# A two-layer decoder trunk on one core: GpSimd applies the gate operands' norm where they are stored, norm factors come two blocks at a time, and layer B's first weights are loaded and split another way

## The chip, the cores and the metric

The kernel runs on one core of one Trainium2 chip. Its engines are PE (TensorE matmul), PEld (its weight load), DVE (VectorE), ACT (ScalarE), POOL (GpSimd) and SP (SyncE, which here issues the DMAs). The metric is the device time of one execution in microseconds (us); the kernel before took 2546.34 us, the median of 3 runs.

## What is computed

2048 tokens of width 1024 go through two layers. Cut to what matters here:

```python
u = rmsnorm(x, norm_a_g)                       # layer A
q, k, v, f, gate = split(u @ w_in_a)           # widths 1024, 1024, 1024, 16, 1024
q, k = rmsnorm per head of 64 (q), (k)
o = fox_attention(q, k, v, log_sigmoid(f + b_forget))      # 16 heads, causal
h = x + (o * silu(gate)) @ w_out_a
k_s, v_s = split(rmsnorm(h, kv_norm_g) @ w_kv)             # 4 heads, shared keys and values
q, gate = split(rmsnorm(h, norm_b_g) @ w_in_b)             # layer B
o = swa_sink_attention(rope(rmsnorm(q)), rope(rmsnorm(k_s)), v_s, sinks)   # window 128
out = h + (o * silu(gate)) @ w_out_b
```

## The kernel before

Every matrix product is made in three matmuls: each operand is split into a high part of type fp32r and a low part with the rest, and high x high, high x low and low x high are added up in one PSUM bank. The norm of x has two factors. The gain of a column is multiplied into the weights when these are split (L396 on ACT makes `wh`, L397 on DVE makes `wl` from the raw weights in a slot of `wr`). The factor of a row, one over the root of the mean square, is not multiplied into x: it is kept in `factors` and applied to each product after the matmul.

`normer` (L478) loads x in 16 blocks of 128 tokens (`load_block`, slots of `st` and `wr` in turn), splits them into `uh` and `ul` (tiles of `big`) and works out the factor of each block: squares, a sum, and in `rstd` (L295) the steps L301 to L307, one set for each block.

`projections` makes layer A's products in seven groups of 6 or 8 heads (4 in the sixth): in each, all weights of the group are loaded and split, and a loop over the 16 blocks runs 24 matmuls (L663) into one of three banks `b`, norms the heads (`qk_norm`: L409 on ACT, L411, L301 to L307, L413 and L415 on DVE; L415 reads the bank last), transposes them on PE (L291, one block later) and stores them. The first group holds half of the values, the second and third the keys, the fourth to sixth the queries (the fourth also the forget gate), the seventh the other half of the values.

Layer A's gate isn't among the groups. Its product is made later, as filler work inside attention, so the groups carry `jobs` for it: in the second and third group its 1024 columns of weights are split and stored (`split_w`, 8 jobs), and in the fourth to seventh `uh` and `ul` are stored to `ut` in DRAM (`spill_u`, 16 jobs of one DMA of 1 MB each). A group does four jobs, at the blocks of `JOBS_AT`.

`attention_a` goes through 16 heads and four chunks of 512 queries. `gate` is a generator that `feed` advances by some matmuls at each step: for each chunk and each of 8 tiles of 128 gate columns it runs 24 matmuls L960 into the bank `pb` (in the tail into `sc`), from `ut` (slots `wh`, `wl`) and the stored weights (`wr`). Then L967 on DVE multiplies the bank by the row factors (`rows`, loaded from `rr` in DRAM), L968 on ACT takes tanh, L969 on DVE makes (1 + tanh) x product, and L970 stores it to `gt`. As the factor is in the product only once this way, the other place of silu's argument is made good elsewhere: `recips`, which inverts the sums of the softmax, multiplies them by the same factors (L816). A flag, `rest`, keeps `feed` still for one step after each gate tile. Attention's own DVE work is the running sums (L914), row maxima (L851, L856) and sums (L801); POOL subtracts high parts from weights of the softmax (L903).

`out_a` makes layer A's output projection: four chunks of 512 tokens, in each two halves of columns and four tiles of 128 tokens, with 24 matmuls L1171 and an evacuation L1175 that adds the residual (a slot of `qn`), stored to `h1` by L1176. While a chunk runs, `gated` multiplies the next chunk's attention output, sums and gate (L1122 on POOL, L1123, L1124 and L1126 on DVE). In the last chunk `last()` loads and splits layer B's first weights (`w_kv`: four loads L379 into `wr`, eight splits L396 and L397), and `norm` begins with the blocks of `h1`: a block is loaded, squared and summed on ACT (L503), transposed on PE (L291, in a bank of `b`) and split (L327, L328).

The order of the instructions on each engine comes from a scheduler that goes by priority, the pools' free slots and its own estimates; some instructions are held in program order.

Of the kernel before, what the change touches and what calls it, by code (L numbers as in the profile page):

```python
# [22 lines left out]
P = 128  # L23
S = 2048
D = 1024
# [33 lines left out]
JOBS_AT = (0, 3, 6, 9)  # L59
# [17 lines left out]
SLOTS = dict(big=8, st=4, wr=2, wh=9, wl=9, sq=2, qn=2, rows=1, rot=1, ro1=1, ro2=2)  # L77
# [13 lines left out]
class Trunk:  # L91
# [56 lines left out]
    def constants(self):  # L148
# [66 lines left out]
        self.gk16 = row("gk16", a["knorm_b_g"].rearrange("(o d) -> o d", o=1)[:, :ROT], ROT)  # L215

        self.late = [self.loads.pop()]
# [120 lines left out]
    def block_sums(self, sums, tb):  # L338

        nc = self.nc  # L340
        ps = self.ps(("pa", "pb")[tb % 2], [P, 1])
        self.tc.keep_in_program_order(
            nc.tensor.matmul(ps, sums, self.ones[:, :1], start=True, stop=True)
        )
# [11 lines left out]
    def weights(  # L356
# [16 lines left out]
        for dt in dts:  # L373
# [20 lines left out]
            else:  # L394
                g = gain[:, dt : dt + 1]
                nc.scalar.activation(h, raw, AF.Copy, scale=g)  # L396
                nc.vector.scalar_tensor_tensor(lo, raw, g, f_(h), ALU.mult, ALU.subtract)  # L397
# [4 lines left out]
        return hs, ls  # L402

    def qk_norm(self, ps, nh, tb, rope, r0):
# [5 lines left out]
        sm = self.sb("sm", [P, 4, 8], bufs=3)  # L410
# [50 lines left out]
    def factor_rows(self, i, ch):  # L461

        rows = self.sb("rows", [P, CH])
# [16 lines left out]
    def normer(self, src):  # L480
# [3 lines left out]
        uh, ul, blocks = {}, {}, {}  # L484
# [10 lines left out]
        def rstd(tb, sm, ss=None):  # L495
            self.rstd(sm, 1, D, ss=ss, out=factors[:, tb : tb + 1])

        def load(tb):
            blocks[tb] = xt = self.load_block(src, tb)
            if not turned:  # L500
                _, junk = parts(tb)
                sm = self.sb("sm", [P, 4, 8], bufs=3)
                nc.scalar.activation(  # L503
                    junk, xt.rearrange("p (c t) -> p c t", t=P), AF.Square,
                    accum_out=sm[:, 0, :1],
                )
                rstd(tb, sm)
# [14 lines left out]
        def factor(tb, dt):  # L522
            if turned and dt == 0:
                blocks[tb] = self.block_squares(blocks[tb])
            if turned and dt == FACTOR_AT:
                sm = self.sb("sm", [P, 4, 8], bufs=3)
                rstd(tb, sm, self.block_sums(blocks.pop(tb), tb))
# [3 lines left out]
    def projections(self, normed, groups, row, later=None, pre=None, hook=None, first=None):  # L531
# [45 lines left out]
        if later is not None:  # L577
            wg, cg, gain, spill, wsplit = later

            def spill_u(ch, k, c0):  # L580
                t = (uh, ul)[k]
                c = slice(c0, c0 + NDT // 2)
                tc.keep_in_program_order(
                    nc.sync.dma_start(
                        out=spill[ch, k, c].rearrange("c p t -> p c t"), in_=f_(t[ch][:, c])
                    )
                )

            def split_w(dt):
# [13 lines left out]
                partial(spill_u, ch, k, c0)  # L603
                for ch in range(NCH) for k in range(2) for c0 in (0, NDT // 2)
# [148 lines left out]
    def attention_a(self, w_out, result):  # L753
# [16 lines left out]

        factors = self.sb("ro1", [NCH * NSB, 2, 32])
# [34 lines left out]
        def recips(h, c0=0, c1=NCH):  # L806
# [9 lines left out]
            nc.vector.tensor_tensor(rc, rc, factors[:nr, 1 if c0 else 0], ALU.mult)  # L816
# [125 lines left out]
        def gate():  # L942


            for ch in range(NCH):
                rows, us = self.factor_rows(0, ch), []
# [4 lines left out]
                for ft in range(NDT):  # L951
# [15 lines left out]
                    nc.vector.tensor_tensor(g, ps, rows, ALU.mult)  # L967
                    nc.scalar.activation(g, g, AF.Tanh, scale=0.5)  # L968
# [18 lines left out]
        for c in range(2):  # L987
            nc.sync.dma_start(
                out=factors[: (NCH - c) * NSB, c],
                in_=d["rr"][0, c * CH :].rearrange("(b i) -> b i", i=32),  # L990
            )
# [17 lines left out]
        gate_bank, weight_slots, rest = "pb", cycle(["wr"]), False  # L1009
# [21 lines left out]
        def feed(n, pause=False):  # L1031


            nonlocal fed, rest
            if pause and rest:
                rest = False
# [445 lines left out]
```

## Time and profile before

| | |
|---|---|
| time, median of 3 runs | 2546.34 us (2545.75 to 2551.03) |
| profiled execution, its own time | 2548.29 us |
| its span, first to last instruction | 2546.4 us |
| mean granted TensorE clock | 0.993 |
| POOL busy | 938.7 us, 611 instructions |
| DVE busy | 1788.7 us, 4353 instructions |

The views used below: the page gives the busy time of each engine over the span, and the span in 40 slices with the busy share of each in tenths. A table of windows gives for each stretch its length, then the busy us (and instructions) of PE, PEld, DVE, ACT and POOL, the granted clock, the share of DMA and GB/s. A row of the timeline holds start, duration (of all that are put together), engine, line, operation, output <- input by the program's names, shape, how often, and in brackets the idle time before with what ended it. A group's row holds how often, then the busy us and the mean ns of one, then the idle time before by what ended it. A row of waits holds the total in us, how often, and the longest.

### The profile page before, as it was taken

The page shows a single profiled execution, that of the slowest core. Times are in us where ns is not written, and L with a number is a line of the kernel's source. Part 1 is how long each engine was busy: PE and PEld are TensorE (multiplying, and loading weights), DVE is VectorE, ACT ScalarE, POOL GpSimd, SP SyncE. Part 2 cuts the span into 40 slices and gives each one's busy share as a digit, 9 for nine tenths or more (in the row PEclk, how much of TensorE's full clock was granted, in tenths as well). Part 3 has the DMA queues.
Part 4 walks back from the last instruction along what each step waited for, and adds up shares of the span by engine and source line. Part 5 has one row for each costly group of instructions (what it writes and reads, how often), then busy time and mean ns, then how long its engine had stood idle before and what let it go on. Part 6 is the DMA issues. An engine that isn't in the chain of part 4 may idle for free. (4 is left out here: it accounts for less than half of the span.)

```text
span 2546.4 us, 37588 instructions
## 1 busy us (share of the span) xinstructions
PE 2474.7 (97%) x12320; PEld 2058.7 (81%) x12320; DVE 1788.7 (70%) x4353; ACT 1350.7 (53%) x2598; POOL 938.7 (37%) x611
## 2 busy tenths in 40 slices
PE   8999999999999999999999899989999999899999
PEld 6788899988878778877887677778888888688887
DVE  7656666726888889888888864436766422788885
ACT  5433333415777778777877631135332213777774
POOL 0000000014877778777877732200011000355552
PEclk9999999999999999999999999999999999999999
DMA  6656655687454654655466478845443424655541
GB/s 190 185 160 187 176 149 147 203 262 226 125 165 118 195 170 137 183 159 159 124 178 182 144 231 262 269 146 151 131 114 94 145 95 139 192 156 163 169 143 65
DMA packets 357155, 419.33 MB, mean 165 GB/s; under 512 B 65440, under 2 KB 248768, under 8 KB 350784
## 3 DMA queue, kind: packets, MB, share of 16 engines
q1 hardware_dynamic: 356960, 416.93, 56.0%
q8 instruction: 98, 1.61, 0.3%
q14 instruction: 97, 0.79, 0.1%
HBM read 265.29 MB, written 151.40 MB: 164 GB/s over the span
## 5 line engine op out<-in xcount | busy, mean ns | idle before, releaser
L663 PE MATMUL b<-wh,big 128*128 128x512 f32 (+3 forms) x2560 | 774.3, 376 | 13.2 <-ACT wh L396 12.8
L903 POOL TENSOR_TENSOR big<-st,big 128x1024 fp32r<-128x1024 f32 (+1 forms) x320 | 678.2, 2132 | 254.3 <-ACT big L902 164.6
L663 PEld LDWEIGHTS b<-wh,big 128*128 128x128 f32 x2560 | 473.9, 189 | 84.2 <-ACT wh L396 14.2
L663 PE MATMUL b<-wl,big 128*128 128x512 f32 (+3 forms) x1280 | 475.7, 372 | 1.1 <-DVE wl L397 0.9
L914 DVE TENSOR_TENSOR ac<-ac,st 128x512 f32<-128x512 f32 (+3 forms) x576 | 355.0, 616 | 48.4 <-ACT ac L906 23.9
L897 ACT ACTIVATE st<-sc 128x512 f32<-128x512 f32 (+1 forms) x512 | 277.4, 586 | 120.0 <-PE sc L889 71.2
L929 PE MATMUL pa<-big 128*128 128x512 f32 (+2 forms) x1280 | 333.0, 373 | 4.3 <-ACT sq L937 3.9
L902 ACT CAST big<-st 128x1024 fp32r<-128x1024 f32 (+1 forms) x320 | 302.5, 946 | 7.7
L663 PEld LDWEIGHTS b<-wl,big 128*128 128x128 f32 x1280 | 242.6, 190 | 37.4 <-DVE wl L397 4.9
L929 PEld LDWEIGHTS pa<-big 128*128 128x128 f32 x1280 | 225.0, 190 | 43.5 <-ACT sq L937 10.2
L888 PE MATMUL sc<-big 128*128 128x512 f32 (+2 forms) x640 | 246.1, 385 | 3.2 <-ACT st L897 1.9
L409 ACT ACTIVATE sq<-b,r 128x512 f32<-128x512 f32 (+2 forms) x128 | 77.8, 608 | 314.5 <-PE b L663 314.4
L889 PE MATMUL sc<-big 67*128 67x512 f32 (+2 forms) x640 | 236.3, 369 | 0.0
L851 DVE CUSTOM_DVE_ANT_0 mx<-mx,rot 128x128 f32<-128x128 f32 (+3 forms) x240 | 210.8, 878 | 34.9 <-PE mx L840 30.3
L840 PE MATMUL mx<-big 66*128 66x128 f32 (+3 forms) x660 | 189.4, 360 | 8.9 <-DVE mt L851 7.1
L1171 PE MATMUL b<-big 128*128 128x512 f32 x768 | 181.4, 397 | 11.7 <-DVE qn L1175 9.0
L1171 PEld LDWEIGHTS b<-big 128*128 128x128 f32 x768 | 145.8, 191 | 46.2 <-DVE qn L1175 10.9
L411 DVE TENSOR_REDUCE sm<-sq 128x8 f32<-128x512 f32 (+2 forms) x128 | 74.9, 585 | 145.2 <-ACT sq L409 144.9
L960 PE MATMUL pb<-wh,wr 128*128 128x512 f32 x448 | 162.3, 400 | 4.1 <-DMA wr<-wg 3.4
L1253 POOL TENSOR_TENSOR st<-st,rs 128x1024 f32<-128x1024 f32 (+1 forms) x64 | 118.4, 1851 | 111.2 <-DVE rs L1252 85.8
L628 PE MATMUL b<-big,wh 128*128 128x512 f32 x512 | 158.4, 390 | 0.7 <-DVE st L634 0.7
L763 POOL MEMSET rot<- 128x1024 bf16 x1 | 1.0, 952 | 426.3 <-PE pb L291 426.3
(245 smaller groups left out, 4307.4 us busy)
## 6 DMA issues: line engine op xcount, KB each, us to landing
wr<-wg SPq DMA_DIRECT2D x60, 512.0 KB, 4.5
va<-st SPq DMA_DIRECT2D x32, 512.0 KB, 3.6
ka<-st SPq DMA_DIRECT2D x64, 256.0 KB, 3.6
ut<-big SPq DMA_DIRECT2D x16, 1024.0 KB, 7.3
big<-ka SPq DMA_DIRECT2D x16, 1024.0 KB, 5.4
big<-qa SPq DMA_DIRECT2D x16, 1024.0 KB, 7.6
qb<-st SPq DMA_DIRECT2D x64, 256.0 KB, 3.8
big<-qb SPq DMA_DIRECT2D x16, 1024.0 KB, 7.3
```

The costliest lines, as they stand in the source:

```text
L663: nc.tensor.matmul(ps[:, :n], u[tb // 4][:, dt, us], W[k][dt], start=(dt == 0 and i == 0), stop=(dt == NDT - 1 and i == 2),)
L840: mm = nc.tensor.matmul(ps[:, b, :wb], qb[:66, i * P : (i + 1) * P], kb[:66, k0 + b * wb : k0 + (b + 1) * wb], start=True, stop=True,)
L851: nc.vector.tensor_tensor_reduce(out=lg, in0=lg, in1=mask, scale=1.0, scalar=NEG, op0=ALU.add, op1=ALU.max, accum_out=f_(o),)
L888: nc.tensor.matmul(o, ka[:, ks], qa[:, qs], start=not (last and n_), stop=False)
L889: nc.tensor.matmul(o, kb[:, ks], qb[:, qs], start=False, stop=not diag)
L897: nc.scalar.activation(pf[:, off : off + w], ps[:, :w], AF.Exp, scale=HD**-0.5)
L902: nc.scalar.copy(ph[:, :tw], pf[:, :tw])
L903: nc.gpsimd.tensor_tensor(pl[:, :tw], pf[:, :tw], f_(ph[:, :tw]), ALU.subtract)
L914: nc.vector.tensor_tensor(a_, a_, pf[:, off : off + w], ALU.add)
L929: nc.tensor.matmul(pv[:, q0 : q0 + w], v[:, k, :], src[:, off : off + w], start=(p == 0 and n_ == 0 and i == 0), stop=(last and n_ == 1 an ...
L960: nc.tensor.matmul(ps, w[:, dt // 2 % 2, wk, dt % 2, :], us[dt][uk], start=(dt == 0 and i == 0), stop=(dt == NDT - 1 and i == 2),)
L1171: nc.tensor.matmul(ps, y[p // 4][:, k, p % 4, ts_], W[nh][j][p], start=(p == 0 and i == 0), stop=(p == NDT - 1 and i == 2),)
```

## The change

**The spill.** A job now takes a quarter of a chunk's `uh` and `ul`: POOL adds the two in a slot of `wr`, multiplies by the row factors (loaded into a slot of `qn`), ACT makes the high part in a slot of `st`, POOL subtracts it, and two DMAs of 512 KB store both parts. So `ut` holds x already normed. In `gate` the multiplication L967 goes, and tanh reads the bank; in `recips` L816 goes; the flag `rest` goes.

**The factors.** `factor` and `load` in `normer` work on two blocks at once: one set of the steps of `rstd` for two blocks.

**Layer B's first weights.** `weights_ahead` loads them as a generator: its four loads (two into `wr`, two into `st`) are put ahead of the last chunk, and one split behind each of its eight tiles.

**Slots.** `qn` has 3 slots instead of 2 and takes over `rows`; the last four blocks of x or h1 are loaded into `st` alone; one small gain (`gk16`) is loaded later, into `part`; the jobs are at blocks 1, 4, 7 and 10.

```diff
-JOBS_AT = (0, 3, 6, 9)
+JOBS_AT = (1, 4, 7, 10)
-SLOTS = dict(big=8, st=4, wr=2, wh=9, wl=9, sq=2, qn=2, rows=1, rot=1, ro1=1, ro2=2)
+SLOTS = dict(big=8, st=4, wr=2, wh=9, wl=9, sq=2, qn=3, rot=1, ro1=1, ro2=2)
...
-        xt = self.sb(("st", "wr")[tb % 2], [P, D])
+        xt = self.sb("wr" if tb % 2 and tb < NTB - 4 else "st", [P, D])
...
+    def weights_ahead(self, src, g, hs, ls):
+        raws = []
+        for dt in range(0, NDT, 2):
+            raws.append(self.sb("wr" if dt < NDT // 2 else "st", [P, 2, CH]))
+            self.nc.sync.dma_start(
+                out=raws[-1], in_=src[dt * P : (dt + 2) * P, :CH].rearrange("(k p) c -> p k c", p=P)
+            )
+        yield
+        for dt in range(NDT):
+            h, lo = self.sb("wh", [P, CH], F32R), self.sb("wl", [P, CH], F32R)
+            self.split_weight(h, lo, raws[dt // 2][:, dt % 2, :], g[:, dt : dt + 1])
+            hs.append(h)
+            ls.append(lo)
+            yield
...
         def factor(tb, dt):
+            both = (tb, tb + 1)
+            if tb % 2:
+                return
             if turned and dt == 0:
-                blocks[tb] = self.block_squares(blocks[tb])
-            if turned and dt == FACTOR_AT:
-                sm = self.sb("sm", [P, 4, 8], bufs=3)
-                rstd(tb, sm, self.block_sums(blocks.pop(tb), tb))
+                for b in both:
+                    blocks[b] = self.block_squares(blocks[b])
+            if dt == FACTOR_AT:
+                sm = self.sb("sm", [P, 4, 8], bufs=4) if turned else small[tb]
+                ss = self.block_sums([blocks[b] for b in both], tb) if turned else None
+                self.rstd(sm, 2, D, ss=ss, out=factors[:, tb : tb + 2])
...
-            def spill_u(ch, k, c0):
-                t = (uh, ul)[k]
-                c = slice(c0, c0 + NDT // 2)
-                tc.keep_in_program_order(
+            def spill_u(ch, c0):
+                if c0 == 0:
+                    rows[ch] = self.factor_rows(row, ch)
+                c = slice(c0, c0 + 2)
+                t, hi = self.sb("wr", [P, 2, CH]), self.sb("st", [P, 2, CH])
+                nc.gpsimd.tensor_tensor(t, f_(uh[ch][:, c]), f_(ul[ch][:, c]), ALU.add)
+                nc.gpsimd.tensor_tensor(
+                    t, t, rows[ch].unsqueeze(1).to_broadcast([P, 2, CH]), ALU.mult
+                )
+                nc.scalar.copy(r_(hi), t)
+                nc.gpsimd.tensor_tensor(r_(t), t, hi, ALU.subtract)
+                for k, part in enumerate((hi, t)):
                     nc.sync.dma_start(
-                        out=spill[ch, k, c].rearrange("c p t -> p c t"), in_=f_(t[ch][:, c])
+                        out=spill[ch, k, c].rearrange("c p t -> p c t"), in_=part
                     )
-                )
...
-            nc.vector.tensor_tensor(rc, rc, factors[:nr, 1 if c0 else 0], ALU.mult)
...
-                    nc.vector.tensor_tensor(g, ps, rows, ALU.mult)
-                    nc.scalar.activation(g, g, AF.Tanh, scale=0.5)
+                    nc.scalar.activation(g, ps, AF.Tanh, scale=0.5)
...
-            if pause and rest:
-                rest = False
-                return
...
-            if not more:
-                given = last()
...
+                    if (ch, nh, tb) == (NCH - 2, 1, 3) or not more:
+                        next(last)
```

On POOL, in layer A's projections, before (L152 to L181 are constants of the start; L763 to L760 set up attention's operands; L903 is attention):

```order
L152 AFFINE_SELECT band<-band 128x128 x2
L763 MEMSET rot 128x1024
L764 AFFINE_SELECT rot<-rot 128x128
L759 MEMSET big 3x2048
L760 MEMSET big 3x2048
```

and after, from the same constant on, with the rows that end the norms (L610 is the addition, L611 the multiplication by the factors, L615 the subtraction):

```order
L152 AFFINE_SELECT band<-band 128x128 x2
L610 TENSOR_TENSOR wr<-big 128x1024 x2
L611 TENSOR_TENSOR wr<-wr,qn 128x1024 x2
L615 TENSOR_TENSOR wr<-wr,st 128x1024 x2
L610 TENSOR_TENSOR wr<-big 128x1024
L611 TENSOR_TENSOR wr<-wr,qn 128x1024
L610 TENSOR_TENSOR wr<-big 128x1024
L611 TENSOR_TENSOR wr<-wr,qn 128x1024
L615 TENSOR_TENSOR wr<-wr,st 128x1024 x2
```

48 operations of 128x1024 stand where there were none, often two jobs of three interleaved; attention's L790 and L791 (L759 and L760 before) stand behind some of them.

On SP, around the start of the output projection's last chunk, before (L1161 loads a residual, L1176 stores a tile of h1, L379 loads layer B's first weights, L315 a block of h1):

```order
L1176 DMA h_68<-qn 128x512
L1161 DMA qn<-in_x 128x512
L379 DMA wr<-in_w_kv 128x2x512
L1161 DMA qn<-in_x 128x512
L379 DMA wr<-in_w_kv 128x2x512
L1176 DMA h_68<-qn 128x512
L315 DMA st<-h_68 128x1024
L1176 DMA h_68<-qn 128x512
L379 DMA wr<-in_w_kv 128x2x512 x2
```

and after (the same lines are L1180, L1195, L407 and L312):

```order
L1195 DMA h_68<-qn 128x512
L1180 DMA qn<-in_x 128x512 x2
L407 DMA wr<-in_w_kv 128x2x512 x2
L1195 DMA h_68<-qn 128x512 x2
L407 DMA st<-in_w_kv 128x2x512 x2
L1180 DMA qn<-in_x 128x512 x2
L312 DMA st<-h_68 128x1024
```

The third and fourth load stand behind the same stores as before, but go to slots of `st`; the loads of h1 follow them. On DVE at the same place, before (numbers behind b_ name the bank's tile; b_16055 is the last tile of the third chunk):

```order
L1175 TENSOR_TENSOR qn<-b_16026,qn 128x512
L1126 TENSOR_TENSOR big<-st,big 128x512
L397 SCALAR_TENSOR_TENSOR wl<-wr,g_kv,wh 128x512
L1175 TENSOR_TENSOR qn<-b_16055,qn 128x512
L397 SCALAR_TENSOR_TENSOR wl<-wr,g_kv,wh 128x512 x3
L301 TENSOR_SCALAR sm<-sm 128x1
```

and after (L1194 is the evacuation, L421 the split, b_16051 the third chunk's last tile, b_16088 and b_16121 the first two of the last chunk):

```order
L1194 TENSOR_TENSOR qn<-b_16022,qn 128x512
L1143 TENSOR_TENSOR big<-st,big 128x512
L1194 TENSOR_TENSOR qn<-b_16051,qn 128x512
L421 SCALAR_TENSOR_TENSOR wl<-wr,g_kv,wh 128x512 x4
L421 SCALAR_TENSOR_TENSOR wl<-st,g_kv,wh 128x512 x3
L1194 TENSOR_TENSOR qn<-b_16088,qn 128x512
L1194 TENSOR_TENSOR qn<-b_16121,qn 128x512
L421 SCALAR_TENSOR_TENSOR wl<-st,g_kv,wh 128x512
```

The third chunk's last evacuation has no split ahead of it any more; the two after it have seven splits ahead instead of eight.

On PE, from the last matmul of one gate tile on (L960 in `pb`; the others are attention's scores, values and maxima), before:

```order
L960 MATMUL pb<-wh,wr 128x512
L888 MATMUL sc<-big 128x512
L889 MATMUL sc<-big 128x512
L888 MATMUL sc<-big 128x512
L889 MATMUL sc<-big 128x512
L929 MATMUL pa<-big 128x512
L840 MATMUL mx<-big 128x512 x2
L929 MATMUL pa<-big 128x512 x3
L888 MATMUL sc<-big 128x512
L889 MATMUL sc<-big 128x512
L888 MATMUL sc<-big 128x512
L889 MATMUL sc<-big 128x512
```

and after, up to the next tile's first matmul (L988 is the gate's line):

```order
L988 MATMUL pb<-wh,wr 128x512
L916 MATMUL sc<-big 128x512
L917 MATMUL sc<-big 128x512
L916 MATMUL sc<-big 128x512
L917 MATMUL sc<-big 128x512
L957 MATMUL pa<-big 128x512
L868 MATMUL mx<-big 128x512 x2
L957 MATMUL pa<-big 128x512 x3
L988 MATMUL pb<-wh,wr 128x512
```

After, the next tile's first matmul stands ten matmuls behind the tile's last one; before, a further step of scores, values and maxima begins there, and the next tile comes behind that.

More of the change, by code (lines that the diff above doesn't have):

```diff
@@ L602, in projections @@
             jobs += [
[L603 to L604 removed]
+                partial(spill_u, ch, c0) for ch in range(NCH) for c0 in range(0, NDT, 2)
             ]
@@ L1404, in layer_a @@
         normed = self.normer(d["h1"])
-        first = self.out_a(
+        first = [], []
+        self.out_a(
             w_out, x, d["h1"], result[:2], result[2], normed[0],
-            partial(self.weights, a["w_kv"], 0, CH, self.g_kv),
+            self.weights_ahead(a["w_kv"], self.g_kv, *first),
         )
```

60 lines of the change are left out of this document (28 added, 32 removed).

## The prediction

> **What bounds the kernel now.** I read the page first, then the idle time before TensorE, then the stretches where the edits stand.
>
> ```profile
> PE 2474.7 (97%) x12320; PEld 2058.7 (81%) x12320; DVE 1788.7 (70%) x4353; ACT 1350.7 (53%) x2598; POOL 938.7 (37%) x611
> POOL 0000000014877778777877732200011000355552
> ```
>
> PE is busy 97% of the span, so an edit elsewhere pays only where PE waits. POOL's row of slices is zero up to attention: layer A's projections, where the new norms go, have the idlest POOL. The table of windows gives the room that DVE has there (columns: length, then busy us of PE, PEld, DVE, ACT, POOL).
>
> ```profile
> 384.00:446.00 62.00, 62.00 (x377) 61.17 (x376) 43.23 (x153) 22.64 (x48) 1.25 (x2) 1.00 0.50 145
> 454.00:500.00 46.00, 46.00 (x388) 45.99 (x388) 34.95 (x139) 17.35 (x48) 0.00 (x0) 1.00 0.72 207
> 1350.00:1400.00 50.00, 45.65 (x220) 35.73 (x219) 45.94 (x81) 36.23 (x59) 37.48 (x19) 1.00 0.57 160
> ```
>
> In the fifth and sixth groups of the projections (first two rows) PE never waits, and DVE has 30% and 24% to spare. At the end of attention (third) DVE is full and PE loses 4.4 of 50 us: time taken off DVE can pay there. The longest single stall is at the start of the last chunk of layer A's output projection. Timelines of PE, DVE, ACT and SP:
>
> ```profile
> 1654.73 2.89 PE L1171 MATMUL b<-big 128*128 128x512 f32 x12
> 1657.46 1.03 PE L291 MATMUL b<-ident,st 128*128 128x128 f32 x8
> 1666.00 8.21 PE L1171 MATMUL b<-big 128*128 128x512 f32 x26 [7.51 <-DVE qn L1175]
> ...
> 1650.92 0.68 DVE L1126 TENSOR_TENSOR big<-st,big 128x512 fp32r<-128x512 f32 x1
> 1653.66 0.69 DVE L1175 TENSOR_TENSOR qn<-b,qn 128x512 f32<-128x512 f32 x1 [0.52 <-DMA qn<-in_x]
> 1656.21 1.41 DVE L397 SCALAR_TENSOR_TENSOR wl<-wr,g_kv,wh 128x512 fp32r<-128x512 f32 x2 [1.21 <-ACT wh L396]
> 1663.93 1.41 DVE L397 SCALAR_TENSOR_TENSOR wl<-wr,g_kv,wh 128x512 fp32r<-128x512 f32 x2 [1.78 <-ACT wh L396]
> 1665.26 1.28 DVE L1175 TENSOR_TENSOR qn<-b,qn 128x512 f32<-128x512 f32 x2
> ...
> 1663.17 1.33 ACT L396 ACTIVATE wh<-wr,g_kv 128x512 fp32r<-128x512 f32 x2 [1.92 <-DMA wr<-in_w_kv]
> ...
> 1655.03 3.00 SPq L379 DMA_DIRECT2D wr<-in_w_kv  x2
> ```
>
> PE waits 7.51 us for the evacuation L1175, which stands on DVE behind the last two splits L397; those wait for ACT's L396, and that for the fourth load of layer B's first weights. SP sat 3.00 us over the last two loads, because the two wr slots came free only when the splits of 1656.21 ended (1657.62). The fourth load needs 1657.6 to 1663.2, 5.5 us. After the stall 26 matmuls take 8.21 us; by the row of 12 (2.89) they would take 6.2, so a slower pace costs 2.0 more. The stall with its tail is 9.5 us.
>
> **The output projection's last chunk.** After, the third and fourth loads take st slots instead of waiting for wr. In the order of instructions they follow the store of the tile that L1175 evacuates at 1653.66. That evacuation had waited 0.52 for its residual and stood behind a split; with three qn slots and no split ahead it follows L1126 at 1651.6. Its store goes at 1652.4 and the loads at about 1653; 5.5 us later it is 1658.5. The seventh split then takes one ACT and one DVE step (0.67 and 0.7, halves of the x2 rows), the evacuation 0.69: the bank is free near 1660.6. PE asks for it when the transposes end, 1657.46 + 1.03 = 1658.5. So some 2 us of 7.5 remain, less if the gating before it also runs earlier; a short stall I charge no slow pace. Gain 8.5 with the gating a little earlier, 5 to 10. The eighth split stands behind the next two evacuations and holds nobody.
>
> **The end of attention.** PE's waits between 1340 and 1500 and two groups of DVE in 1350 to 1500, then the store in the way:
>
> ```profile
> PE mx L840 <- DVE mt L851: 7.1, 4, 2.5
> PE sc L960 <- DMA st<-wg: 5.1, 1, 5.1
> ...
> L816 DVE TENSOR_TENSOR sq<-sq,ro 64x32 f32<-64x32 f32 (+2 forms) x4 | 3.2, 791 | 0.0
> L967 DVE TENSOR_TENSOR sq<-pb,rows 128x512 f32<-128x512 f32 x4 | 2.7, 671 | 0.0
> ...
> 1478.74 0.67 DVE L969 SCALAR_TENSOR_TENSOR sq<-sq,pb 128x512 f32<-128x512 f32 x1
> ...
> 1479.44 0.32 SPq L970 DMA_DIRECT2D gt<-sq  x1
> ```
>
> L816 and L967 go: 3.2 + 2.7 = 5.9 us off a DVE that PE waited on for 7.1. Where DVE is 92% busy I let three quarters through, 4.5. The gate weights st<-wg, for which PE waits 5.1, stand on SP behind the store of 1479.44, and that waited for L969; without L967 ahead of it, it goes at least 0.68 earlier, say 1. Gain 5.5; none if POOL or ACT is late next, 9 if all of it and more of the SP queue passes.
>
> **The gate tiles inside attention.** One tile's end and the next one's start, which use the same bank:
>
> ```profile
> 749.82 0.39 PE L960 MATMUL pb<-wh,wr 128*128 128x512 f32 x1
> ...
> 752.68 0.63 ACT L968 ACTIVATE sq<-sq 128x512 f32<-128x512 f32 x1
> ...
> 753.34 0.69 DVE L969 SCALAR_TENSOR_TENSOR sq<-sq,pb 128x512 f32<-128x512 f32 x1 [0.18 <-ACT sq L968]
> 754.38 0.39 PE L960 MATMUL pb<-wh,wr 128*128 128x512 f32 x1
> ```
>
> The bank was free at 754.0, 3.8 us after the tile; PE came at 754.4, one step skipped by the flag that is removed. After, PE comes after as few as ten matmuls, 2.4 us by the row of 12. Tanh (0.63) and L969 (0.69) need 1.3 plus two queues; read straight from the bank they end 1.6 to 2.7 after the tile. So 0.3 us can be lost on some of 28 tiles, while DVE is rid of L967 and L816 all through. I take a gain of 1, between 4 gained and 3 lost.
>
> **Layer A's projections: what the norms cost.** 48 POOL operations of 128x1024 come, 16 CASTs on ACT, and 32 stores of half the size for 16. Nearest prices, and what DVE does beside such operations:
>
> ```profile
> L903 POOL TENSOR_TENSOR big<-st,big 128x1024 fp32r<-128x1024 f32 x192 | 461.3, 2408 | 133.3 <-ACT big L902 78.9 <-PE sc L889 31.0 <-PE pa L929 11.1
> L1253 POOL TENSOR_TENSOR st<-st,rs 128x1024 f32<-128x1024 f32 x60 | 114.3, 1904 | 77.5 <-DVE rs L1252 72.8 <-DVE nm L1240 3.3 <-DVE es L1243 1.4
> ...
> 712.39 5.72 POOL L903 TENSOR_TENSOR big<-st,big 128x1024 fp32r<-128x1024 f32 x3 [0.67 <-ACT big L902]
> ...
> 715.55 1.35 DVE L816 TENSOR_TENSOR sq<-sq,ro 64x32 f32<-64x32 f32 x1
> 716.83 1.21 DVE L856 TENSOR_REDUCE mt<-mx 128x1 f32<-128x1024 f32 x1
> ...
> 1486.22 0.18 DVE L816 TENSOR_TENSOR sq<-sq,ro 48x32 f32<-48x32 f32 x1
> ...
> 1349.28 3.79 POOL L903 TENSOR_TENSOR big<-st,big 128x896 fp32r<-128x896 f32 x2
> ...
> 1349.35 2.59 DVE L1123 TENSOR_TENSOR qn<-qn,wl 128x512 f32<-128x512 f32 x1 [0.96 <-POOL qn L1122]
> L1123 DVE TENSOR_TENSOR st<-st,wr 128x512 f32<-128x512 f32 x24 | 16.6, 692 | 63.3 <-DMA wr<-rd 49.6 <-POOL st L1122 13.7
> ```
>
> The reduction L856, one SBUF input, takes its 1.21 beside a running L903. L816 and L1123, two SBUF inputs each, take 1.35 and 2.59 beside one, 0.18 and 0.69 without: they wait until the POOL operation ends. So a DVE operation with two SBUF inputs that meets a norm on POOL waits for the rest of its 1.9 (L1253's, the nearest: plain f32) to 2.4 us (L903's).
>
> The Trainium skill, GPSIMD Engine Reference, section 8 (Key points), says that GpSimd shares its SBUF interfaces with VectorE, with "contention with DVE instructions in a 2-port perf mode or with two SBUF inputs". The rows agree for two inputs; the sum below is the same by it. That one-input operations of a 2-port mode would wait too, no row here shows; it would cost more than I charge.
>
> In the projections the two-input operations are three steps of each query block's rstd (L304, L305, L307) and the weight splits L397. The change from group to group, DVE and PE:
>
> ```profile
> L304 DVE TENSOR_TENSOR sm<-sm x160: 146/166/170, 21.9 to 2000.6; 128x8 f32<-128x8 f32 x64, 128x1 f32<-128x1 f32 x32, 128x6 f32<-128x6 f32 x32, 128x4 f32<-128x4 f32 x32
> ...
> 378.74 0.61 DVE L397 SCALAR_TENSOR_TENSOR wl<-wr,g_a,wh 128x384 fp32r<-128x384 f32 x1
> 380.13 0.62 DVE L397 SCALAR_TENSOR_TENSOR wl<-wr,g_a,wh 128x384 fp32r<-128x384 f32 x1 [0.70 <-ACT wh L396]
> ...
> 380.80 0.44 PE L663 MATMUL b<-wl,big 128*128 128x384 f32 x1 [0.21 <-DVE wl L397]
> ```
>
> PE here waits for the seventh split the moment it ends (380.75). The first norm of a group takes the wr slot that the sixth split frees at 379.35, so its addition runs on POOL from then to 381.3 or 381.8, and the seventh split cannot end before 381.9 to 382.4: 1.2 to 1.7 us late, 2.4 if the addition starts later. Four such changes: 6, from 5 to 9.6.
>
> Inside the fourth and fifth groups the 30% of spare DVE time covers the waits: nothing, unless rival 2. In the sixth a block is 2/3 as long, DVE has 24% spare, and POOL runs its operations in bursts of six (about 12 us, two in this group): some eight chains of three two-input steps meet one or two remainders of about 1 us each, 8 to 16 us in all, of which spare time and the three PSUM slots hide most; I charge 4, from 1 to 9. In the seventh group the weight loads share their two wr slots with the norms, and SP's queue stands behind stores that wait for POOL: 2, from 0 to 5. At the start of attention POOL's memsets of its operands stand behind the last norms: 1, from 0 to 2. Costs 13, from 6 to 26. Covered and charged nothing: the 16 CASTs (ACT 23 of 62 us busy), the pairwise factors (DVE loses half of its rstd steps), the later loads of the key gain.
>
> **Sum.** −8.5 −5.5 −1 +13 = −2. The profiled execution took 2548.29 (span 2546.4 and 1.9 around it), 1.95 over the median of 2546.34; it would become 2546.3, and in terms of the median 2544.
>
> **Rivals.** A difference under 0.2%, 5.1 us, can't be told from none.
>
> 1. The locks mostly miss, cost 4: two-input steps fall between POOL's operations, and sixth and seventh groups hide the rest. For it: PE never waits in the first two windows. −8.5 −5.5 −1 +4 = −11, 2535 (2531 to 2539).
> 2. Slower: POOL holds layer A's DVE. Each chain of L304, L305, L307 meets a new POOL operation at each step, as L1123 did, 3 x 1.9 = 5.7 us per block; where a block lasts 3.1 us (the second window's 388 matmuls in 46 us, 26 to a block with its transposes), DVE falls behind, the evacuation L415 that follows the chain frees its bank late, and PE waits. It decides once a burst costs PE over 4 us, since two bursts, the four changes and the SP queue then pass 18. With 6 more per burst and 3 more on the changes the costs are 28: −15 + 28 = +13; between, at +10, it is 2556 (2549 to 2560). Against it: 48 operations of 1.9 to 2.4 are 91 to 115 us in the 290 of the four groups, so two blocks in three meet none. By the skill's section above this is the rule at its strictest.
> 3. The change doesn't remove the stall: the four loads land no sooner than 1663.2 because DMA is shared with the stores, and the bank comes at 1665 as before. −8.5 becomes −1, the sum +6, 2552.
>
> **How the numbers follow.** Forecast 0.40 (−7 to +3), rival 1 0.29, rival 2 0.25, rival 3 0.06. The range runs from rival 1's lower end, 2531, to rival 2's upper part, 2558; the forecast's own is 2539 to 2549. Faster by over 5.1: rival 1 and a quarter of the forecast, 0.39. Slower: 0.20 of rival 2, 0.04 of rival 3, none of the forecast, rounded up for the overlap to 0.26. Within: the rest, 0.35.
>
> **What would show it.** Right: POOL operations of about 1.9 us from 300 to 590; a seventh split near 2 us in the four changes; no PE wait over 3 us at the output projection's last chunk, with the third and fourth loads on st slots not waiting for a split; DVE-ended waits at the end of attention halved. Wrong: PE losing under 4 or over 20 us in the four last groups; L304 at its 0.17 beside POOL operations (then the lock is not there); or the stall still 7 us.

## The result: slower by half a per cent

The changed kernel takes 2561.1 us (median of 7 runs, 2554.34 to 2571.17) against 2547.1 before (7 runs, 2542.17 to 2551.03): a ratio of 1.0052, 95% interval 1.0031 to 1.0074. That is 14 us slower, 3 above the range's upper end.

The profiled execution of the changed kernel was the longest of its seven (2571.17; span 2569.5), so it lies 23.1 us over the span of before where the medians are 14.0 apart. The stages below are read from it. The page of the changed kernel:

```profile
PE 2477.6 (96%) x12320; PEld 2065.1 (80%) x12320; DVE 1808.8 (70%) x4224; ACT 1364.3 (53%) x2599; POOL 1053.7 (41%) x659
POOL 0000124351877777877777732200011000355552
```

PE's busy time is nearly the same; POOL has 115 us more, all in the slices ahead of attention; DVE has 129 instructions fewer and yet 20 us more. Where the time went is seen by following the same matmul in both traces (the first of each stage, by its number among those of its line):

| stage | before, us | after, us | longer by |
|---|---|---|---|
| groups one to three | 0 to 301.3 | 0 to 295.3 | −6.0 |
| group four | 301.3 to 376.2 | 295.3 to 378.9 | +8.7 |
| group five | 376.2 to 451.8 | 378.9 to 466.9 | +12.5 |
| group six | 451.8 to 501.5 | 466.9 to 535.3 | +18.7 |
| group seven | to 598.9 | to 632.0 | −0.7 |
| attention, to three quarters of its values | to 1253.0 | to 1281.5 | −4.6 |
| the rest of attention and of the gate | to 1507.5 | to 1533.7 | −2.5 |
| output projection | to 1703.4 | to 1727.4 | −2.1 |
| layer B | to the end | to the end | −0.9 |

Groups five and six in the table of windows (length, busy us of PE, PEld, DVE, ACT, POOL, then the clock, DMA share and GB/s), before:

```profile
376.00:452.00 76.00, 75.77 (x457) 74.05 (x457) 53.11 (x182) 30.52 (x66) 1.25 (x2) 1.00 0.55 160
452.00:501.50 49.50, 49.50 (x417) 49.30 (x415) 38.32 (x147) 20.62 (x56) 0.00 (x0) 1.00 0.70 206
```

and after:

```profile
378.00:467.00 89.00, 78.79 (x462) 75.85 (x460) 73.16 (x184) 35.32 (x71) 29.94 (x14) 0.98 0.48 142
467.00:535.00 68.00, 53.71 (x414) 52.77 (x413) 56.70 (x144) 22.99 (x58) 28.56 (x12) 0.90 0.51 148
```

For the same work DVE's busy time went from 53 to 73 and from 38 to 57 us, and PE, hardly idle before, is idle for 10 and 14 us. PE's own busy time grew too, from 75.8 to 78.8 and from 49.5 to 53.7 us, at a granted clock of 0.98 and 0.90 instead of 1.00. Over groups four to seven together PE is idle for 31 us instead of 1 and busy for 306 instead of 297 at a granted clock of 0.97: of the 39.2 us lost there, 30 are waits and 9 are slower matmuls. What DVE is busy with shows one stretch of group six, timelines of DVE, POOL and PE:

```profile
482.70 1.68 DVE L298 TENSOR_SCALAR sm<-sm 128x4 f32<-128x4 f32 x1
484.66 0.18 DVE L300 RECIPROCAL sm<-sm 128x4 f32<-128x4 f32 x1 [0.27 <-ACT sm L299]
484.87 1.84 DVE L301 TENSOR_TENSOR sm<-sm 128x4 f32<-128x4 f32 x1
486.75 2.26 DVE L302 SCALAR_TENSOR_TENSOR sm<-sm 128x4 f32<-128x4 f32 x1
489.04 2.26 DVE L304 SCALAR_TENSOR_TENSOR sm<-sm 128x4 f32<-128x4 f32 x1
...
481.95 4.74 POOL L611 TENSOR_TENSOR wr<-wr,qn 128x1024 f32<-128x1024 f32 x2 [6.52 <-DMA qn<-rr]
486.63 4.66 POOL L615 TENSOR_TENSOR wr<-wr,st 128x1024 fp32r<-128x1024 f32 x2
...
492.63 0.66 PE L288 MATMUL pa<-ident,qn 128*128 128x128 f32 x2 [7.43 <-DVE st L458]
```

Four steps of one block's rstd, 128x4 elements each, take 1.68, 1.84, 2.26 and 2.26 us beside four POOL operations in a row: each step waits for one of them to end, and while it runs POOL begins the next. L300, the reciprocal, is not held. L458, which empties the bank of the transposes, stands on DVE behind these steps (at 492.01), and PE waits 7.4 us for it. This is rival 2, step for step. The change from group four to five shows the other form, a weight split on DVE, the norm's addition on POOL, and PE:

```profile
382.11 2.78 DVE L421 SCALAR_TENSOR_TENSOR wl<-wr,g_a,wh 128x384 fp32r<-128x384 f32 x1
...
382.13 2.35 POOL L610 TENSOR_TENSOR wr<-big 128x1024 f32<-128x1024 f32 x1 [31.57 <-DVE sm L302]
...
384.95 0.44 PE L694 MATMUL b<-wl,big 128*128 128x384 f32 x1 [2.00 <-DVE wl L421]
```

The seventh split starts 0.02 us ahead of the addition in the records and still takes 2.78 instead of 0.62.

### The profile page after: what moved, and what is told of

Read it like the earlier page. It is cut to its first block, busy times and chain, and to the rows that moved or that the text cites. A ratio compares the mean times of both kernels' runs of the same rounds, so it can differ in the third digit from the quotient of the medians.

```text
span 2569.5 us, 37654 instructions
## 1 busy us (share of the span) xinstructions
PE 2477.6 (96%) x12320; PEld 2065.1 (80%) x12320; DVE 1808.8 (70%) x4224; ACT 1364.3 (53%) x2599; POOL 1053.7 (41%) x659
## 5 line engine op out<-in xcount | busy, mean ns | idle before, releaser
L694 PEld LDWEIGHTS b<-wl,big 128*128 128x128 f32 x1280 | 244.0, 191 | 43.6 <-DVE wl L421 11.2
L879 DVE CUSTOM_DVE_ANT_0 mx<-mx,rot 128x128 f32<-128x128 f32 (+3 forms) x240 | 210.8, 878 | 44.7 <-PE mx L868 41.0
L610 POOL TENSOR_TENSOR wr<-big 128x1024 f32<-128x1024 f32 x16 | 38.8, 2422 | 394.0 <-DVE sm L302 350.8
L988 PE MATMUL pb<-wh,wr 128*128 128x512 f32 x448 | 166.3, 401 | 5.3 <-DMA wr<-wg 4.0
```

The source lines that it names most:

```text
L694: nc.tensor.matmul(ps[:, :n], u[tb // 4][:, dt, us], W[k][dt], start=(dt == 0 and i == 0), stop=(dt == NDT - 1 and i == 2),)
L879: nc.vector.tensor_tensor_reduce(out=lg, in0=lg, in1=mask, scale=1.0, scalar=NEG, op0=ALU.add, op1=ALU.max, accum_out=f_(o),)
L988: nc.tensor.matmul(ps, w[:, dt // 2 % 2, wk, dt % 2, :], us[dt][uk], start=(dt == 0 and i == 0), stop=(dt == NDT - 1 and i == 2),)
```

## The experiments

Two theories stood at the start: POOL's running time holds DVE (1), or the norms' slots in `wr` and `st` and their stores on SP's queue do it (2). All runs are of one core; "before" in each is a set of runs of the kernel before on the same chip (medians 2546.5, 2548.2 and 2547.4 for the three sets).

**Short POOL operations.** The three operations of a job cover 16 of 512 columns; ACT copies the low part into the slot, so that every slot, wait and store remains; the gate's operands stay un-normed but for these columns.

```diff
-                nc.gpsimd.tensor_tensor(t, f_(uh[ch][:, c]), f_(ul[ch][:, c]), ALU.add)
+                nc.scalar.copy(t, f_(ul[ch][:, c]))
+                s = slice(0, 16)
+                nc.gpsimd.tensor_tensor(t[:, :, s], f_(uh[ch][:, c, s]), f_(ul[ch][:, c, s]), ALU.add)
...
```

> The changed kernel with POOL's three operations per job on 16 of 512 columns; ACT copies the low part instead, so slots, stores and waits stay (the gate's operands are left un-normed but for these columns). Theory 1, POOL's running time holds DVE: groups four to seven, 39 us longer than before in the profile, return to before's 300 us, and the kernel takes 2515 to 2530 us. Theory 2, the slots of wr and st and the stores on SP's queue cost it: nearly nothing changes, 2555 to 2565.

2520.9 us (2512.8 to 2524.4), ratio 0.9899 (0.9872 to 0.9927). By the same matmuls, groups four to seven take 0.2 us more than before. A POOL operation and two DVE steps (mean in the last but one column):

```profile
L612 POOL TENSOR_TENSOR wr<-big 128x32 f32<-128x32 f32 x16 | 4.0, 253 | 436.3 <-ACT wr L610 367.9 <-DMA qa<-st 25.3 <-DMA wr<-in_w_in_a 24.2
...
L298 DVE TENSOR_SCALAR sm<-sm 128x6 f32<-128x6 f32 x32 | 5.2, 164 | 0.2
L301 DVE TENSOR_TENSOR sm<-sm 128x6 f32<-128x6 f32 x32 | 5.3, 165 | 0.9
```

The instructions stand in nearly the same order (on DVE some twenty of the four groups' 571 stand a few places off), the slots, stores and waits are the same, and the loss is gone. It is POOL's running time. Shorter operations also give the slots back sooner, so this run alone doesn't rule out theory 2 for the whole loss. The DVE steps that take 1.68 to 2.26 us each in the rows above tell against it: by the trace they have started, and wait for no slot.

**Quarter pieces.** Each POOL operation cut into four of 128x256, all work kept.

```diff
-                nc.gpsimd.tensor_tensor(t, f_(uh[ch][:, c]), f_(ul[ch][:, c]), ALU.add)
+                cuts = [(k, slice(i, i + 256)) for k in range(2) for i in range(0, CH, 256)]
+                for k, s in cuts:
+                    nc.gpsimd.tensor_tensor(
+                        t[:, k, s], f_(uh[ch][:, c0 + k, s]), f_(ul[ch][:, c0 + k, s]), ALU.add
+                    )
...
```

> The changed kernel with each POOL operation cut into four of 128x256 (0.7 us each, four times as many, all work kept). Theory 1: a DVE step that meets one waits 0.7 instead of 2.4 us, and gets four times as many gaps, so the cost in groups four to seven falls from 39 to 10 to 15 us: 2530 to 2540. Theory 2: POOL needs longer in sum and the slots are held longer: 2561 to 2570.

2537.4 us (10 runs), ratio 0.9974 (0.9959 to 0.9988): faster than both kernels. Groups four to seven are 18.7 us longer than before, where whole operations made it 39.2, although POOL's work there grew from 115 to 137 us. The size of one operation matters, more than their sum. Of 89 steps of rstd and qk_norm on DVE that start beside a running POOL operation, 88 take at most 0.74 us, one 2.89; with whole operations such a step takes up to 2.46 us (median 1.86). 18.7 is more than the 10 to 15 expected.

**The old slots for blocks of x.** `load_block` as before.

```diff
-        xt = self.sb("wr" if tb % 2 and tb < NTB - 4 else "st", [P, D])
+        xt = self.sb(("st", "wr")[tb % 2], [P, D])
```

> The changed kernel with the blocks of x and h1 loaded into st and wr in turn to the last, as before. The gain of 6 us at the change from the first to the second group was not forecast. Theory: the wr slots that the last blocks leave free let the second group's weights load earlier; then the 6 us are lost again, 2565 to 2568. Rival: it comes from the pairwise factors or the later jobs; then 2559 to 2563.

2566.9 us (2559.3 to 2571.3), ratio 1.0081 (1.0055 to 1.0108). PE at the change from the first group to the second, in before, after and this run:

```profile
111.55 0.80 PE L663 MATMUL b<-wh,big 128*128 128x512 f32 x1 [3.63 <-ACT wh L396]
```

```profile
108.21 0.73 PE L694 MATMUL b<-wh,big 128*128 128x512 f32 x2 [0.19 <-ACT wh L420]
```

```profile
111.00 0.73 PE L694 MATMUL b<-wh,big 128*128 128x512 f32 x2 [3.63 <-ACT wh L420]
```

The wait of 3.63 us is back to the hundredth, and 4.1 of the 6.0 us with it (the same matmul is 1.9 ahead of before instead of 6.0). So most of this unforeseen gain is the last four blocks' slots in `st`: `wr` is free for the second group's weights sooner.

**The old spill.** The norms, the gate's multiplication, L816's and the flag as before, with two slots of `qn` and one of `rows`.

```diff
-                    nc.scalar.activation(g, ps, AF.Tanh, scale=0.5)
+                    nc.vector.tensor_tensor(g, ps, rows, ALU.mult)
+                    nc.scalar.activation(g, g, AF.Tanh, scale=0.5)
...
```

> The changed kernel without its norms on POOL: uh and ul are stored as before, the multiplications by the row factors and the flag after a gate tile are back, and qn has 2 slots and rows 1. Theory 1 and 2 alike: the 39 us go, the 7 us gained in attention go too, the rest of the gains stays: 2529 to 2540. If it is not under 2545, the loss is not the spill's.

2545.9 us (10 runs), ratio 0.9997 (0.9981 to 1.0013): the same as before. Missed by 6, and above the 2545 I had named. Its profile agrees with the loss being the spill's: groups four to seven are 0.3 us longer than before. The rest isn't what I had added up: the 4.6 us gained by group four and the 4.3 in the output projection are offset by attention, 5.3 longer than before with the same code there. In attention the instructions of each engine stand in the same order as before, so no edit accounts for these 5.3 us; their cause stays open.

**Eighth pieces.** The same cut with 128 columns.

> The changed kernel with each POOL operation cut into eight of 128x128 (about 0.46 us each by the profile's 0.74 for 256 and 0.33 for 64 columns). Theory 1, a DVE step waits for one running POOL operation: the cost in groups four to seven falls on, from 39 with whole operations and 19 with quarters to 8 to 14 us, though POOL now works 177 us in all: 2525 to 2535. Rival, the cost follows POOL's total time (115, 142, 177 us): it rises, 2540 to 2550.

2573.2 us (2563.1 to 2575.5), ratio 1.0089 (1.0061 to 1.0117): worse than whole operations, and outside both expectations; groups four to seven are 48.8 us longer than before. DVE and POOL in group four:

```profile
321.14 13.55 DVE L298 TENSOR_SCALAR sm<-sm 128x6 f32<-128x6 f32 x1
...
318.38 6.73 POOL L619 TENSOR_TENSOR wr<-wr,st 128x128 fp32r<-128x128 f32 x16
325.06 3.35 POOL L612 TENSOR_TENSOR wr<-big 128x128 f32<-128x128 f32 x8
328.35 3.36 POOL L616 TENSOR_TENSOR wr<-wr,qn 128x128 f32<-128x128 f32 x8
331.65 3.35 POOL L612 TENSOR_TENSOR wr<-big 128x128 f32<-128x128 f32 x8
```

One DVE step on 128x6 elements takes 13.55 us, over more than thirty POOL operations with no gap between them, and another in group six 10.23. These are exceptions: of 97 steps of this kind that start beside a running POOL operation, 94 take at most 0.53 us, so as a rule DVE gets in between two. The two long waits together are 24 us.

**Norms on DVE.** The same work as 96 operations of 128x512 on DVE.

```diff
-                nc.gpsimd.tensor_tensor(t, f_(uh[ch][:, c]), f_(ul[ch][:, c]), ALU.add)
+                for k, s in cuts:      # 512 columns each
+                    nc.vector.tensor_tensor(
+                        t[:, k, s], f_(uh[ch][:, c0 + k, s]), f_(ul[ch][:, c0 + k, s]), ALU.add
+                    )
...
```

> The changed kernel with the 48 operations as 96 of 128x512 on DVE instead of POOL: no lock, but 96 x 0.69 = 66 us more for DVE in 300 us of which it has some 85 free. If only the lock cost time, groups four to seven take what they took before plus up to 10 us: 2525 to 2535. If DVE's room was the true limit: 2540 to 2560.

2530.0 us (2528.3 to 2533.5), ratio 0.9928 (0.9909 to 0.9948). Group five in the table of windows, and one of the new operations:

```profile
371.50:451.00 79.50, 76.83 (x456) 75.10 (x454) 64.46 (x206) 33.83 (x70) 1.59 (x2) 0.98 0.53 155
```

```profile
L612 DVE TENSOR_TENSOR wr<-big 128x512 f32<-128x512 f32 x32 | 21.4, 682 | 3.6 <-DMA ut<-wr 3.5
```

With the norms added to its own work DVE is busy 64 of 79.5 us here, against 73 of 89 when POOL does them. Over groups four to seven DVE is busy for 181 us before, 237 with the norms on POOL and 228 with the norms on DVE: it spends 47 us on doing the work and 56 on waiting for POOL to do it. Groups four to seven are 8.4 us longer than before.

**Late splits.** On the quarter pieces: in the last chunk of the output projection the blocks of h1 are loaded first, then layer B's first weights, split two at a time behind the last four tiles.

```diff
-                    if (ch, nh, tb) == (NCH - 2, 1, 3) or not more:
-                        next(last)
                     if ch == NCH - 1 and tb % 2:
                         norm(2 * nh + tb // 2 + 1)
+                    if not more and (nh, tb) == (0, 1):
+                        next(last)
+                    if not more and nh:
+                        next(last)
+                        next(last)
```

> The quarter pieces, and in the output projection's last chunk the blocks of h1 are loaded ahead of layer B's first weights, which are split two at a time behind its last four tiles. Theory: PE's stall of some 5 us there, and the slow matmuls behind it, come from the h1 block's load standing behind the weights and from seven splits ahead of the evacuation; both go: 6 to 7 us under the quarter pieces, 2530 to 2532. Rival, the DMA engines are simply full there: 2536 to 2539.

2535.8 us (2524.4 to 2538.8), ratio 0.9943 (0.9923 to 0.9963). PE at that place:

```profile
1650.96 6.01 PE L1194 MATMUL b<-big 128*128 128x512 f32 x25 [0.82 <-DVE big L1147]
1656.81 1.03 PE L288 MATMUL b<-ident,st 128*128 128x128 f32 x8
1657.60 10.69 PE L1194 MATMUL b<-big 128*128 128x512 f32 x46
```

Behind the transposes no wait is left, and no slow pace. From the last chunk's start to its third tile this kernel is 7.6 us shorter than before, the quarter pieces 2.5, so the order of loads and splits is the cause and the DMA engines were not simply full. How much each of the two moves is worth this run doesn't tell, as it makes both. The median came down by 1.6, less than the 6 to 7 expected; in the profile the 5.1 us gained here are offset by an attention 4.8 longer than that of the quarter pieces, with each engine's instructions in the same order there; no edit explains it.

**Old first weights.** On the quarter pieces, `weights` called at the last chunk's start, as before.

```diff
+            if not more:
+                given = last()
...
-                    if (ch, nh, tb) == (NCH - 2, 1, 3) or not more:
-                        next(last)
```

> The quarter pieces with layer B's first weights loaded and split at the last chunk's start into wr, as before. By the profiles of the changed kernel the new way is worth 2 to 3 us here, not the 8.5 forecast: 2539 to 2541. If the forecast held, 2546.

2542.4 us (12 runs, 2530.8 to 2550.0), ratio 0.9974 (0.9961 to 0.9988), the same ratio as the quarter pieces have with medians 5 apart, and between what was expected of the profiles (2539 to 2541) and of the forecast (2546). By the time this is unclear; in the profiles the place takes 0.4 us less than before here and 2.5 less with the new way. Its order isn't that of the kernel before either: the block of h1 is loaded behind the last weights here too (at 1653.36), and PE's transposes wait for it:

```profile
1659.55 1.94 PE L288 MATMUL b<-ident,st 128*128 128x128 f32 x8 [6.65 <-DMA st<-h]
```

**Both remedies.** Norms on DVE and late splits together.

> The norms on DVE (96 operations of 128x512) together with the late splits of layer B's first weights. If the two gains are independent, the late splits take off what they took at that place in the profile of the quarter pieces, 5 us: 2524 to 2527. If a full DVE shifts the loss elsewhere: 2529 to 2532.

2526.5 us (2525.8 to 2531.1), ratio 0.992 (0.9907 to 0.9934): 21 us under before, and the fastest version that leaves no work out. The late splits take 3.5 us off the median of the norms on DVE, and the median is where the sum was expected. In the profiles the output projection gained 10.1 us against the norms on DVE alone and attention took 9.3 longer, again in the same order of instructions.

**Eighth pieces again.** The label is a slip: this is the kernel of e5 unchanged, for a second profile.

> The eighth pieces once more, unchanged, for a second profile: if one L298 being held over many POOL operations (13.6 and 10.2 us in the first profile) is how DVE meets a run of short operations, it is there again, with 10 us or more in one or two places. If it was a chance, the longest L298 is under 3 us.

2569.6 us, one run. The long waits are there again, L298 taking 10.67 us at the same place and 11.80 in group six, so they were no chance.

**Eighth pieces, L298 on ACT.**

```diff
-        nc.vector.tensor_scalar(v, ss, 1.0 / count, EPS, ALU.mult, ALU.add)
+        nc.scalar.activation(v, ss, AF.Copy, scale=1.0 / count, bias=EPS)
```

> The eighth pieces with the one step L298, a tensor_scalar from SBUF, done by ACT (same result) instead of DVE. Theory: a tensor_scalar is held until POOL's run of operations ends, steps with two SBUF inputs until one operation ends; without L298 the stalls of 10 to 14 us go: 2573 becomes 2535 to 2550. Rival: whatever step comes first after the reduction is held; then L301 takes the long waits and it stays at 2565 to 2575.

2577.4 us (2564.7 to 2580.0), ratio 1.0099 (1.0073 to 1.0125). 2 us above the rival's range. My theory on kinds of steps falls; the next step takes the wait:

```profile
322.48 13.22 DVE L301 TENSOR_TENSOR sm<-sm 128x6 f32<-128x6 f32 x1
335.73 0.37 DVE L302 SCALAR_TENSOR_TENSOR sm<-sm 128x6 f32<-128x6 f32 x1
```

In all three profiles the long wait falls on whichever held step comes first after the reduction; those behind it wait for 0.2 us. The wait doesn't last until POOL's run ends: in the rows of the first profile L298 ends at 334.69, and POOL's operations go on without a gap to 335.00 and beyond. Why one step is passed over some thirty times where most get in at once, and what lets it in at last, no run here shows.

## Why the prediction was wrong

**The cost in layer A, the step that failed.** Forecast +13 with bounds 6 and 26; measured +39.2 in the profile; the medians of e1 and of the changed kernel are 40 apart, over the whole kernel. The mechanism was named and its part "Inside the fourth and fifth groups the 30% of spare DVE time covers the waits: nothing" was wrong: these two lost 21 us, some 17 beside their waits for the seventh split. The sixth group, forecast at 4 and at most 9, lost 18.7, some 17 beside that wait. The size failed in three places. First, the price: I took 1.9 us for a norm, from L1253 as the nearest, and 2.4 from L903 as the other end; POOL's three lines took L903's (L611 2.40 and L615 2.39 us):

```profile
L610 POOL TENSOR_TENSOR wr<-big 128x1024 f32<-128x1024 f32 x16 | 38.8, 2422 | 394.0 <-DVE sm L302 350.8 <-DVE wl L421 24.8 <-DMA ca<-wr 9.4
```

Second, how many steps are held. Groups of DVE steps in groups four and five, before and after:

```profile
L301 DVE TENSOR_SCALAR sm<-sm 128x6 f32<-128x6 f32 x32 | 5.2, 162 | 0.1
L413 DVE TENSOR_SCALAR sm<-sm,r 128x6 f32<-128x6 f32 x32 | 7.4, 231 | 1.0
```

```profile
L298 DVE TENSOR_SCALAR sm<-sm 128x6 f32<-128x6 f32 x32 | 11.8, 368 | 0.2
L432 DVE TENSOR_SCALAR sm<-sm,r 128x6 f32<-128x6 f32 x32 | 11.6, 361 | 1.0
L300 DVE RECIPROCAL sm<-sm 128x6 f32<-128x6 f32 x32 | 5.9, 184 | 5.0 <-ACT sm L299 5.0
```

Two TENSOR_SCALAR steps, which read one tensor from SBUF, are held too, the reciprocal isn't (184 ns; before, 186). Five steps of a chain wait, not three. My row for a step with one SBUF input, L856, doesn't bear on this: it reads a PSUM bank and nothing else. My list also left out the forget gate's steps in the fifth group, of which L781 took 2.63 us (0.42 before). The Trainium skill, GPSIMD Engine Reference, section 8 (Key points), names two cases of contention between GpSimd and VectorE: instructions "in a 2-port perf mode or with two SBUF inputs". The trace agrees for the second (L301 to L304, 1.84 to 2.26 us instead of 0.16). The first, which I had left out of the sum, would cover TENSOR_SCALAR; that these steps run in such a mode no run shows.

Third, the averaging. I let a chain meet "one or two remainders of about 1 us". Since the jobs of POOL come two at a time, four operations run without a gap, and each step of a chain meets a new one and waits nearly its whole length (1.84, 2.26, 2.26). That was rival 2, weighed against by POOL's share of the time. The share says how many blocks are hit, not what a hit costs: the block above lost some 7 us (the four rows less 0.16 each) where a block lasts 3.1, and PE waited 7.4. The kernel before had already shown two steps in a row that each meet a new operation, DVE and POOL at the end of attention:

```profile
1452.24 2.87 DVE L1123 TENSOR_TENSOR qn<-qn,wl 128x512 f32<-128x512 f32 x1 [1.82 <-POOL qn L1122]
1455.51 2.39 DVE L1124 TENSOR_TENSOR qn<-qn 128x512 f32<-128x512 f32 x1
...
1452.17 5.17 POOL L903 TENSOR_TENSOR big<-st,big 128x1024 fp32r<-128x1024 f32 x2
```

Both take 0.69 us when nothing holds them. Last, I charged slower matmuls behind a wait at the output projection alone; in these groups they are 9 of the 39.2 us.

**The four changes of group** were forecast at 6; PE's waits for the seventh split were 1.8, 2.0 and 1.9 us in three of them, 5.7 in all. **The seventh group** lost nothing of the 2, **attention's start** nothing of the 1.

**The end of attention.** Forecast −5.5, measured −2.5 in this profile. DVE's part went somewhat further than the 4.5 forecast, from 8.1 us (L851 7.1, L856 1.0) to 2.4 (now L879 and L884), and other waits come next. PE's waits there, after:

```profile
PE pa L957 <- POOL big L931: 4.1, 2, 3.7
PE pa L957 <- ACT sq L965: 3.5, 1, 3.5
PE sc L988 <- DMA st<-wg: 3.1, 1, 3.1
...
PE mx L868 <- DVE mt L884: 1.5, 2, 1.0
PE mx L868 <- DVE mt L879: 0.9, 1, 0.9
```

The gate weights' wait fell from 5.1 to 3.1, more than the 1 forecast. How good the 5.5 was one profile can't tell. Ten other profiles, e1 to e3 and e5 to e11, have the same instructions in the same order on every engine in attention, and their gain here lies between 5.1 and 11.2 us. The table of windows for before, after and the quarter pieces (e2):

```profile
1253.00:1507.50 254.50, 233.85 (x1093) 184.85 (x1092) 217.39 (x357) 175.60 (x277) 177.98 (x86) 0.97 0.60 171
```

```profile
1281.50:1533.70 252.20, 236.01 (x1093) 188.25 (x1093) 207.79 (x340) 175.81 (x277) 178.93 (x86) 0.95 0.60 171
```

```profile
1260.30:1504.10 243.80, 230.16 (x1093) 182.94 (x1093) 206.77 (x341) 176.69 (x278) 180.45 (x86) 0.99 0.61 177
```

PE's idle time fell from 20.6 to 16.2 and 13.6 us; the rest of the difference is its busy time, 2.2 more than before in the changed kernel and 3.7 less in e2, at granted clocks of 0.97, 0.95 and 0.99. What set the clock apart in the same order of instructions stays open.

**Mid attention** gave 4.6 where I took 1 and named 4 as its upper end; in the same ten profiles it gave 0 to 4.8.

**The output projection.** Forecast −8.5, measured −2.1, and 2.4 at the place itself. PE, then DVE, ACT and SP of the changed kernel there:

```profile
1677.67 6.00 PE L1190 MATMUL b<-big 128*128 128x512 f32 x25 [0.32 <-DVE big L1143]
1688.37 1.94 PE L288 MATMUL b<-ident,st 128*128 128x128 f32 x8 [4.69 <-DVE qn L1194]
...
1685.05 2.09 DVE L421 SCALAR_TENSOR_TENSOR wl<-st,g_kv,wh 128x512 fp32r<-128x512 f32 x3 [1.99 <-ACT wh L420]
1687.06 1.28 DVE L1194 TENSOR_TENSOR qn<-b,qn 128x512 f32<-128x512 f32 x2
...
1688.34 1.06 ACT L521 ACTIVATE big<-st 128x1024 fp32r<-128x1024 f32 x1 [1.36 <-DMA st<-h]
...
1678.68 0.97 SPq L407 DMA_DIRECT2D st<-in_w_kv  x2
1681.73 0.45 SPq L312 DMA_DIRECT2D st<-h  x1
```

The path that I followed came out: the chunk starts at 1671.98, and the evacuation of its first tile ends near 1687.7, 15.7 us later, where I had 15.0. What I had not costed is a DMA that the weights were moved ahead of: the block of h1, issued in before at 1651.46 in front of the last weights, comes at 1681.73 behind them. PE's transposes need it. I let them run during the wait, as before; they start with ACT's square of the same block, at 1688.34, so PE waits 4.69 us and then runs them at half speed (1.94 us; 1.03 before). PE's row names L1194, whose second run ended in the same moment; ACT's row names the block's DMA, as PE's own row does in e8. So the third tile begins at 1689.96, where its bank was free at 1687.7, and the slower pace behind the stall, 2.0 of the 8.5, stays. e7, with the block ahead of the weights and the splits behind the tiles, has no such wait.

**What I charged at nothing.** The blocks' slots gave 4 of the 6 us gained ahead of group four (e3).

The rivals: 2 happened, and beyond the 28 at which I had priced it; 1 didn't; 3 partly, with another transfer as the one that is late. In rival 2 the sum that was to "pass 18" is 16 by its own terms (two bursts of 4, the changes at 6, the SP queue at 2).

## What to carry to other kernels

GpSimd is not free room while DVE works from SBUF: list the DVE steps that read two operands from SBUF (and TENSOR_SCALAR) in the stretch, and price one POOL operation's whole length for each, for as long as POOL's operations run without a gap; the spare share of DVE's time, 24 and 30% here, says little. Cutting POOL's operations helped at a quarter and hurt at an eighth, and doing the same work on DVE was better than either. When a load is moved, look at each load that falls behind it, and place work that nobody waits for (here weight splits) behind the evacuations on the same engine, not ahead of them. And a term of a few us can't be judged by one profile: eleven with the same order of instructions differ by 8.7 us at the end of attention.

## What was not expected of the hardware

A DVE step of 128x6 elements took 13.55, 10.67 and 13.22 us beside gapless POOL operations of 0.46 us, though 94 of 97 such steps took at most 0.53 us in the first of these profiles; beside operations of 2.4 us no such step took more than 2.46. The same norm took POOL 2.39 to 2.42 us per 128x1024 against 0.68 per 128x512 on DVE.
